# Merge gates and branch projections with tokens on the output's partitions, 512 weight columns moving

## The chip, the cores and the metric

The kernel runs on one core of a Trainium2 chip. The engines of that core work beside each other and are ordered by semaphores: TensorE (PE, matrix products; its weight loads are listed as PEld), VectorE (DVE), ScalarE (ACT), GpSimd (POOL) and SyncE (SP), which here issues every DMA. The metric is the device time of the whole kernel in microseconds, the median over runs.

## The reference

One layer of a hybrid block over 256 latent tokens and 256 context tokens of width 2048, in float32. The input is normalised and modulated, then one large projection feeds three mixers: neighbourhood attention, multi-scale pooling, and a two-directional RWKV-7 scan. Each mixer's 1024 channels are multiplied by SiLU of a gate. What the change touches is the end of the layer:

```python
b_na = y_na.astype(dt) * jax.nn.silu(keep(na_gate))
b_pool = y_pool.astype(dt) * jax.nn.silu(keep(pool_gate))
b_rw = y_rw.astype(dt) * jax.nn.silu(keep(rw_gate))
g_na, g_pool, g_rw = jnp.split(jax.nn.sigmoid(keep(merge_logits)), N_BRANCH, axis=-1)
merged = g_na * (b_na @ w_branch[0]) + g_pool * (b_pool @ w_branch[1]) + g_rw * (b_rw @ w_branch[2])
out = merged @ w_out
return x_lat + gate_l[:, None] * out, None
```

The merge logits are 3 x 2048 columns of the input projection, each branch projection is 1024 by 2048, the output projection 2048 by 2048. A final normalisation follows.

## The kernel before

Every float32 product is made of three products in a faster format: an operand is split into a rounded high part (a copy on ACT) and the rest (a subtraction on DVE), and high x high, high x low and low x high are summed in PSUM. The weights are split on the way: `split_unit` (L563) loads 128x512 values into a `raw` tile (7 buffers), and makes `whi` and `wlo` of it (5 buffers each). The normalised input lies split in 16 + 16 tiles, `hh` and `hl`, with channels on partitions and 512 tokens along the row (the latent ones are 256 to 511).

Four stages follow each other. The start makes the modulation and the first tiles. The mixers run up to about 1330 us: a table `todo` of column tiles (`column_tile`, L718) feeds attention, pooling and the scan. A column tile computes 128 output channels for 256 or 512 tokens: the weights are the stationary operand, the tokens move, in four units of 12 products. The 48 tiles of the merge logits depend on nothing and stand last in the table, so they fill PE whenever no other tile is ready; `merge_out` (L827) writes the tanh of each to memory (`md_`). The order of the work on PE is written out by the class `Order`: it keeps a clock of its own, runs the steps of attention and scan when their inputs should be there, and otherwise takes the next product of a unit from `units()` (L1008), which keeps three units loaded ahead. After the last attention step, 64 pieces of the gate weights `w_mg` (256 KB each, `wg`, L958) are loaded, one with each unit, and multiplied on PE in between (`mg`, L970).

Each finished branch piece (128 channels, 256 tokens) is stored to memory by `keep` (L764). The third stage reloads all three branches, 1 MB each through one buffer, and splits them (L1044 to L1048). Then, for each of 16 blocks of 128 output channels and each of the 3 branches, 24 products (`mm3`, L573) with the weights stationary and 256 tokens moving make the projection `br`; DVE multiplies by the gate (tanh + 1) and adds. The sum comes out with channels on partitions, as the output projection needs it (`mh`, `ml`). The last stage, the output projection, keeps tokens stationary and moves 512 columns of `w_out`; its weights reuse `hh` and `hl`.

Of the kernel before, what the change touches and what calls it, by code (L numbers as in the profile page):

```python
# [531 lines left out]
def hybrid_block(ctx, tc, x, cx, w_ms, w_st, w_in, w_mg, w_br, w_out, pool_w, icnt, wa, bias, rows, params, out, dbg=None):  # L532
# [20 lines left out]
    md_ = drp.tile([48, P, NT], F32, name="md_")  # L553
    bs = drp.tile([3, 8, P, NT], F32, name="bs")

    hh = [hp.tile([P, 512], F32R, name=f"hh{j}") for j in range(16)]
    hl = [hp.tile([P, 512], F32R, name=f"hl{j}") for j in range(16)]
# [4 lines left out]
    def split_unit(src):  # L562
# [3 lines left out]
        nc.sync.dma_start(raw, src)  # L566
# [6 lines left out]
    def mm3(acc, a, b, start, stop):  # L573

        nc.tensor.matmul(acc, a[0], b[0], start=start, stop=False)  # L575
        nc.tensor.matmul(acc, a[0], b[1], start=False, stop=False)  # L576
        nc.tensor.matmul(acc, a[1], b[0], start=False, stop=stop)  # L577
# [170 lines left out]
    with ExitStack() as mx:  # L748
# [15 lines left out]
        def keep(br, p, b):  # L764
            nc.sync.dma_start(bs[br, p], b)
# [61 lines left out]
        def merge_out(i, d):  # L827
            th = wp.tile([P, NT], F32, tag="th", bufs=1, name=f"mth{i}")
            nc.scalar.activation(th, d, AF.Tanh, scale=0.5)
            nc.sync.dma_start(md_[i], th)  # L830
# [174 lines left out]
        for i in range(48):  # L1005
            todo.append((None, tile_(MERGE + i, True, merge_out, i)))

        def units():  # L1008

            ready, cur, gates = [], [], gate_units()  # L1010
            while True:
                while len(ready) < AHEAD:
                    if not cur:
                        i = next((i for i, (ev, _) in enumerate(todo) if ev is None or O.has(ev)), None)
                        if i is None:
                            break
                        cur = todo.pop(i)[1]()
# [11 lines left out]

        O.add(side(), 0)  # L1030
# [5 lines left out]
    mark(nc, "bload")  # L1036
    bp = ctx.enter_context(tc.tile_pool(name="bp", bufs=1, reuse_waits="tile"))
    bx = ExitStack()
    bq = bx.enter_context(tc.tile_pool(name="bq", bufs=1, reuse_waits="tile"))
    tp = bx.enter_context(tc.tile_pool(name="tp", bufs=2, reuse_waits="tile"))  # L1040
    bh, bl = [], []
    for br in range(3):
        f = tp.tile([P, 8, NT], F32, tag="bf", bufs=1, name=f"bf{br}")
        nc.sync.dma_start(f, bs[br].rearrange("k p t -> p k t"))  # L1044
        h_ = bq.tile([P, 8, NT], F32R, name=f"bh{br}")
# [144 lines left out]
```

## Time and profile before

| | |
|---|---|
| time, median of 3 runs | 1597.64 us (1594.66 to 1600.06) |
| profiled execution: its time, its span | 1594.74 us, 1593.0 us |
| busy: PE, PEld, DVE, ACT, POOL | 1520.5, 1309.4, 1132.3, 815.9, 242.3 us |
| from the first to the last product on gate weights | 1178.7 to 1324.8 us |
| branch projections, from the first product to the output projection | 1350.9 to 1497.1 us |
| bytes moved, mean rate | 283.28 MB, 178 GB/s |

Times of the profile are microseconds from the span's start. A matrix product is drawn longer than its share of the engine, since products are pipelined; what one costs is seen from the distance of the starts. The DMA share is the mean busy share of the 16 DMA engines of the core.

### The profile page before, as it was taken

Reading aid. Unit: us, or ns where it says so; the run is one execution under the profiler, and the core shown is the slowest. Engines: PE = TensorE matmul, PEld = TensorE weight load, DVE = VectorE, ACT = ScalarE, POOL = GpSimd, SP = SyncE. Lnnn points to the kernel's source line nnn. Section 1 sums busy time; section 2 is a strip of 40 time slices with the busy share of each in tenths; the row PEclk is TensorE's granted clock in tenths of the full one; section 3 lists DMA queues with packets and bytes.
Section 4 is the critical chain, followed back from the end, with each engine's and each line's share of the span. In section 5 each row is a group of like instructions: output and inputs, shape, how many; then the busy total and the mean of one; then the engine's idle time right before and its main releaser. Section 6 shows DMA issues by size and latency. Waiting matters only on the chain.

```text
span 1593.0 us, 36719 instructions
## 1 busy us (share of the span) xinstructions
PE 1520.5 (95%) x13976; PEld 1309.4 (82%) x13976; DVE 1132.3 (71%) x2585; ACT 815.9 (51%) x1606; POOL 242.3 (15%) x441
## 2 busy tenths in 40 slices
PE   6999999999999999999999999899998999899997
PEld 4667788988887988888888887787887778899987
DVE  4224787898787787779779777777984444677774
ACT  5224653664664564366466446535743344444553
POOL 2222100330220150022024103002310200000000
PEclk9999999999999999999999999999999999999999
DMA  9997454435433544433434452443378788777882
GB/s 381 339 330 231 142 161 141 149 113 172 124 118 122 148 125 130 146 98 107 133 124 130 140 161 63 126 129 123 112 226 244 246 272 263 225 233 232 280 301 73
DMA packets 209809, 283.28 MB, mean 178 GB/s; under 512 B 67808, under 2 KB 114016, under 8 KB 205024
## 3 DMA queue, kind: packets, MB, share of 16 engines
q1 hardware_dynamic: 209632, 280.93, 55.1%
q8 instruction: 110, 1.80, 0.5%
q14 instruction: 67, 0.55, 0.1%
HBM read 262.24 MB, written 18.35 MB: 176 GB/s over the span
## 4 chain that ended last, share of the span: by engine, by line
PE 78%; DVE 9%; DMA 5%; ACT 4%; issue 2%; POOL 1%; SPq 1%; ACTq 0%; DVEq 0%; POOLq 0%
PE d L739 43%; PE br L575 3%; PE br L577 3%; PE br L576 3%; PE acc L663 2%; PE psm L615 2%; PE o L577 2%; PE o L575 2%; PE o L576 2%; DMA wg<-in_w_mg 2%; PE acc L669 2%; PE acc L666 2%; DVE wlo L570 1%; PE pu L388 1%; DMA bf<-bs 1%
## 5 line engine op out<-in xcount | busy, mean ns | idle before, releaser
L569 ACT CAST whi<-raw 128x512 fp32r<-128x512 f32 x584 | 358.5, 620 | 445.8 <-PE d L739 307.3
L739 PE MATMUL d<-hh,whi 128*128 128x256 f32 (+1 forms) x1952 | 578.7, 320 | 0.7 <-ACT whi L569 0.7
L739 PE MATMUL d<-hl,whi 128*128 128x256 f32 (+1 forms) x1952 | 552.4, 306 | 0.0
L570 DVE TENSOR_TENSOR wlo<-raw,whi 128x512 fp32r<-128x512 f32 x584 | 405.0, 701 | 176.1 <-ACT whi L569 123.5
L739 PEld LDWEIGHTS d<-hh,whi 128*128 128x128 f32 x1952 | 368.4, 189 | 44.1 <-issue 11.7
L739 PEld LDWEIGHTS d<-hl,whi 128*128 128x128 f32 x1952 | 369.3, 189 | 19.2 <-issue 1.6
L739 PE MATMUL d<-hh,wlo 128*128 128x256 f32 (+1 forms) x1952 | 362.3, 306 | 2.0 <-DVE wlo L570 2.0
L739 PEld LDWEIGHTS d<-hh,wlo 128*128 128x128 f32 x1952 | 286.6, 189 | 20.9 <-DVE wlo L570 2.4
L370 POOL TENSOR_SCALAR sg<-SV,G 64x64 f32<-64x64 f32 x192 | 108.3, 569 | 280.0 <-DVE SV L407 138.2
L575 PE MATMUL br<-bh,whi 128*128 128x256 f32 x384 | 108.9, 284 | 5.6 <-ACT bh L1047 5.6
L576 PE MATMUL br<-bl,whi 128*128 128x256 f32 x384 | 108.7, 283 | 1.5 <-DVE bl L1048 1.5
L577 PE MATMUL br<-bh,wlo 128*128 128x256 f32 x384 | 108.6, 283 | 0.0
L575 PEld LDWEIGHTS br<-bh,whi 128*128 128x128 f32 x384 | 73.3, 191 | 6.0 <-ACT bh L1047 5.8
L576 PEld LDWEIGHTS br<-bl,whi 128*128 128x128 f32 x384 | 73.2, 191 | 1.7 <-DVE bl L1048 1.7
L577 PEld LDWEIGHTS br<-bh,wlo 128*128 128x128 f32 x384 | 73.2, 191 | 0.0
L309 DVE TENSOR_TENSOR iM<-iA,iT 128x126 f32<-128x126 f32 (+22 forms) x248 | 63.4, 256 | 12.7 <-DMA iA<-dA 6.2
L311 DVE TENSOR_TENSOR iT<-iT,iM 128x126 f32<-128x126 f32 (+22 forms) x248 | 63.6, 257 | 6.6
L676 ACT ACTIVATE hh<-xT,md 128x256 fp32r<-128x256 f32 x32 | 17.5, 593 | 88.9 <-DVE md L635 88.9
L1118 DVE TENSOR_TENSOR hl<-rawo,hh 128x512 fp32r<-128x512 f32 x64 | 42.8, 690 | 21.5 <-ACT hh L1117 21.0
L1117 ACT CAST hh<-rawo 128x512 fp32r<-128x512 f32 x64 | 39.5, 621 | 33.0 <-PE o L577 23.3
L139 POOL MEMSET up<- 128x8 f32 x16 | 1.8, 112 | 345.4 <-PE mp L339 183.9
L624 DVE COPY ms<-psm 128x256 f32<-128x256 f32 x16 | 6.8, 425 | 65.1 <-PE psm L615 65.1
(283 smaller groups left out, 2335.7 us busy)
## 6 DMA issues: line engine op xcount, KB each, us to landing
raw<-in_w_in SPq DMA_DIRECT2D x488, 256.0 KB, 3.4
wm<-in_w_ms SPq DMA_DIRECT2D x32, 1024.0 KB, 6.6
raw<-in_w_br SPq DMA_DIRECT2D x96, 256.0 KB, 3.3
wg<-in_w_mg SPq DMA_DIRECT2D x64, 256.0 KB, 4.1
rawo<-in_w_out SPq DMA_DIRECT2D x64, 256.0 KB, 4.4
wst<-in_w_st SPq DMA_DIRECT2D x16, 448.0 KB, 7.3
md__79<-mth SPq DMA_DIRECT2D x48, 128.0 KB, 2.9
mth<-md__79 SPq DMA_DIRECT2D x48, 128.0 KB, 3.1
```

What stands on the lines that cost most here:

```text
L309: nc.vector.tensor_tensor(m, A[:, st:st + 1, st + 1:32].to_broadcast([128, ni, nt]), T[:, 0:ni, st:st + 1].to_broadcast([128, ni, nt]), AL ...
L311: nc.vector.tensor_tensor(T[:, 0:ni, st + 1:32], T[:, 0:ni, st + 1:32], m, ALU.add)
L370: nc.gpsimd.tensor_scalar(sg[hv[par], d], SV[hv[par], par, w, d], G[hv[par], gs[d][0], d:d + 1], None, ALU.mult)
L569: nc.scalar.copy(h, raw)
L570: nc.vector.tensor_tensor(l, raw, h.bitcast(F32), ALU.subtract)
L575: nc.tensor.matmul(acc, a[0], b[0], start=start, stop=False)
L576: nc.tensor.matmul(acc, a[0], b[1], start=False, stop=False)
L577: nc.tensor.matmul(acc, a[1], b[0], start=False, stop=stop)
L615: mm = nc.tensor.matmul(psm[j][32 * g:32 * g + 32, 0:256], cs[:, kt], wm[:, k], start=(kt < 4), stop=(kt >= 12), tile_position=(0, 32 * g))
L739: nc.tensor.matmul(box[0], w[m >= 8][:, 128 * i:128 * i + 128], x, start=(u == 0 and m == 0), stop=(u == 3 and m == 11))
L1117: nc.scalar.copy(hh[kt], raw)
L1118: nc.vector.tensor_tensor(hl[kt], raw, hh[kt].bitcast(F32), ALU.subtract)
```

## The change

The merge logits and the branch projections now have the output projection's form: 128 tokens are stationary, 512 weight columns move, and the results have tokens on partitions. A `group` is one block of 512 output channels for both halves of the tokens. It goes through 16 (merge) or 8 (branch) units; each unit is one 128-channel slice of the input with the weights of four neighbouring column tiles (four pieces of 128 columns per partition, out of the unchanged layout in memory). There are 12 merge groups in the place of 48 tiles and 4 groups per branch in the place of 48 blocks. A group holds two PSUM banks, one for each half of the tokens.

`keep` stores the branches already split. They are loaded into the places of the input (`hh`, `hl`) once the last merge group is on its way: those of attention and pooling with its units 7 to 14, those of the scan after its last piece is stored. The sums lie in the last input tiles. The first two branches' groups run as fillers (`late`) inside the mixers' stage; only the scan's branch is left for the stage behind, where four transposes per sum on PE bring it to channels on partitions. The gate weights come with two of three units instead of every unit. In `mm3` the second and third product change places.

```diff
-    md_ = drp.tile([48, P, NT], F32, name="md_")
-    bs = drp.tile([3, 8, P, NT], F32, name="bs")
+    md_ = drp.tile([12, 2, P, 512], F32, name="md_")
+    bs = drp.tile([3, 2, 8, P, NT], F32, name="bs")
...
-        nc.sync.dma_start(raw, src)
+        nc.sync.dma_start(raw.rearrange("p (n c) -> p n c", c=128) if len(src.shape) == 3 else raw, src)
...
+    def group(nk, src, st, bank, done):
+        acc, w = [None, None], {}
+        def unit_(k):
+            w[k] = split_unit(src(k))
+            def mult(k, t):
+                if k == 0:
+                    acc[t] = bank(t)
+                x = [a[:, 128 * t:128 * t + 128] for a in st(k)]
+                mm3(acc[t], x, w[k], k == 0, k == nk - 1)
+                if k == nk - 1:
+                    done(t, acc[t])
+                return 0.68
+            seq = [(k, 0)] + [(k - 1, 1)] * (k > 0) + [(k, 1)] * (k == nk - 1)
+            return [lambda a=a: mult(*a) for a in seq]
+        return [lambda k=k: unit_(k) for k in range(nk)]
...
+    def branch_load(i):
+        br, k = i // 4, 2 * (i % 4)
+        for e, y in enumerate((hh, hl)):
+            x = y[i] = hp.tile([P, 512], F32R, tag=f"h{'hl'[e]}{i}", name=f"b{'hl'[e]}{i}")
+            nc.sync.dma_start(x.bitcast(F32).rearrange("p (k t) -> p k t", k=2), bs[br, e, k:k + 2].rearrange("k p t -> p k t"))
+    def branch_src(br, c):
+        return lambda k: w_br[br, 4 * c:4 * c + 4, :, 128 * k:128 * k + 128].rearrange("n p c -> p n c")
...
         def keep(br, p, b):
-            nc.sync.dma_start(bs[br, p], b)
+            h = wp.tile([P, NT], F32R, tag="th", bufs=1, name=f"kh{br}_{p}")
+            nc.scalar.copy(h, b)
+            l = b.bitcast(F32R)
+            nc.vector.tensor_tensor(l, b, h.bitcast(F32), ALU.subtract)
+            nc.sync.dma_start(bs[br, 0, p], h.bitcast(F32))
+            nc.sync.dma_start(bs[br, 1, p], l.bitcast(F32))
...
+        def merge_group(i):
+            src = lambda k: w_in[MERGE + 4 * i:MERGE + 4 * i + 4, :, 128 * k:128 * k + 128].rearrange("n p c -> p n c")
+            return group(16, src, lambda k: (hh[k][:, 256:512], hl[k][:, 256:512]), dbank, lambda t, d: merge_out(i, t, d))
...
-        for i in range(48):
-            todo.append((None, tile_(MERGE + i, True, merge_out, i)))
+        for i in range(12):
+            todo.append((None, lambda i=i: merge_group(i)))
+        late = [lambda br=br, c=c: branch_group(br, c) for br in range(2) for c in range(4)]
...
-                        if O.has("side7") and gates:
-                            cur = [lambda u=u, g=gates.pop(0): u() + g() for u in cur]
                     ready.append(cur.pop(0)())
+                    if free is not None:
+                        if 0 <= free - 7 < 8:
+                            branch_load(free - 7)
+                        if free >= 20 and loads and O.has("rw7"):
+                            branch_load(loads.pop(0))
+                        free += 1
+                    n += 1
+                    if n % 3 and O.has("side7") and gates:
+                        ready[-1] = ready[-1] + gates.pop(0)()
...
-        f = tp.tile([P, 8, NT], F32, tag="bf", bufs=1, name=f"bf{br}")
-        nc.sync.dma_start(f, bs[br].rearrange("k p t -> p k t"))
...
+        def done(t, a):
+            nc.vector.scalar_tensor_tensor(th[t], th[t], 1.0, a, ALU.add, ALU.mult)
+            nc.vector.tensor_tensor(th[t], th[t], merged(t, c), ALU.add)
+            ps = psn.tile([P, 4, P], F32, tag="so"[t], name=f"mt{c}_{t}")
+            for i in range(4):
+                nc.tensor.transpose(ps[:, i], th[t][:, 128 * i:128 * i + 128], ident)
```

PE while gate weights stream, before: `d123` is a merge tile, `whi` and `wlo` the split weights, `hh0` and so on the input, `mg3` the gate products.

```order
L970 MATMUL mg3_17559<-wg3_0_7_17640,cs_74 32x256 x2
L739 MATMUL d123_17713<-hh0_81,whi465_17660 128x256
L739 MATMUL d123_17713<-hl0_97,whi465_17660 128x256
L739 MATMUL d123_17713<-hh1_82,whi465_17660 128x256
L739 MATMUL d123_17713<-hl1_98,whi465_17660 128x256
L739 MATMUL d123_17713<-hh2_83,whi465_17660 128x256
```

The same place in the changed kernel: `dg0` and `dg1` are the two halves of the tokens of a pooling-branch group, `bh5` and `bl5` the branch in the place of the input.

```order
L1043 MATMUL mg3_17419<-wg3_1_3_17622,cs_74 32x256 x2
L575 MATMUL dg0_17593<-whi534_17632,bh6_16832 128x512
L576 MATMUL dg0_17593<-whi534_17632,bl6_16834 128x512
L577 MATMUL dg0_17593<-wlo534_17633,bh6_16832 128x512
L575 MATMUL dg1_17608<-whi533_17618,bh6_16832 128x512
L576 MATMUL dg1_17608<-whi533_17618,bl6_16834 128x512
L577 MATMUL dg1_17608<-wlo533_17619,bh6_16832 128x512
L575 MATMUL dg0_17593<-whi535_17648,bh7_16848 128x512
```

A unit of 12 narrow products has become one of six wide ones, and what fills PE beside the gate products are now mostly branch groups, since more merge work stands ahead of them.

The DMA queue of SP at the same place, before (`raw` is a unit's weights, `md` the tanh going out):

```order
L566 DMA raw_17106<-in_w_in 128x512
L566 DMA raw_17148<-in_w_in 128x512
L830 DMA md__79<-mth_16833 128x256
L958 DMA wg_1_6_16855<-in_w_mg 128x2x256
L958 DMA wg_1_7_16888<-in_w_mg 128x2x256
L566 DMA raw_17169<-in_w_in 128x512
L566 DMA raw_17217<-in_w_in 128x512
L958 DMA wg_0_0_16919<-in_w_mg 128x2x256
```

And of the changed kernel, with the units 7 and following of the last merge group:

```order
L566 DMA raw_16714<-in_w_in 128x4x128
L611 DMA bh_16720<-bs 128x2x256
L611 DMA bl_16722<-bs 128x2x256
L566 DMA raw_16730<-in_w_in 128x4x128
L611 DMA bh_16736<-bs 128x2x256
L611 DMA bl_16738<-bs 128x2x256
L1031 DMA wg_1_0_16740<-in_w_mg 128x2x256
L566 DMA raw_16752<-in_w_in 128x4x128
L611 DMA bh_16758<-bs 128x2x256
L611 DMA bl_16760<-bs 128x2x256
L1031 DMA wg_1_1_16762<-in_w_mg 128x2x256
L566 DMA raw_16770<-in_w_in 128x4x128
```

The weights come in four pieces per partition, and the branch loads, which stood in a stage of their own, share the queue with weights and gate weights.

More of the change, by code (lines that the diff above doesn't have):

```diff
@@ L1028, in units @@
                     yield m()
+        loads = [8, 9, 10, 11]
         O.add(side(), 0)
@@ L1033, in hybrid_block @@
             O.run(units(), MOST, LEAST)
-    mark(nc, "bload")
+        for i in loads:
+            branch_load(i)
+    mark(nc, "merge")
     bp = ctx.enter_context(tc.tile_pool(name="bp", bufs=1, reuse_waits="tile"))
[L1038 to L1042, printed above, removed]
-        f = tp.tile([P, 8, NT], F32, tag="bf", bufs=1, name=f"bf{br}")
-        nc.sync.dma_start(f, bs[br].rearrange("k p t -> p k t"))
-        h_ = bq.tile([P, 8, NT], F32R, name=f"bh{br}")
-        l_ = bq.tile([P, 8, NT], F32R, name=f"bl{br}")
-        nc.scalar.copy(h_, f)
-        nc.vector.tensor_tensor(l_, f, h_.bitcast(F32), ALU.subtract)
-        bh.append(h_)
-        bl.append(l_)
+    bx = ctx.enter_context(tc.tile_pool(name="bx", bufs=2, reuse_waits="tile"))
@@ new lines, in last_branch, with done @@
+    def last_branch(c):
+        th = []
+        for t in range(2):
+            th.append(bx.tile([P, 512], F32, tag=f"mth{t}", name=f"mth{c}_{t}"))
+            nc.sync.dma_start(th[t], md_[8 + c, t])
+        def done(t, a):
+            nc.vector.scalar_tensor_tensor(th[t], th[t], 1.0, a, ALU.add, ALU.mult)
[3 more added lines that the diff above has]
+                nc.tensor.transpose(ps[:, i], th[t][:, 128 * i:128 * i + 128], ident)
+            o = (slice(None), slice(4 * c, 4 * c + 4), slice(128 * t, 128 * t + 128))
+            nc.scalar.activation(mh[o], ps, AF.Copy, scale=0.5)
+            nc.vector.scalar_tensor_tensor(ml[o], ps, 0.5, mh[o].bitcast(F32), ALU.mult, ALU.subtract)
+        pool_, tag = ((psd, "d"), (psf, "f"))[c % 2]
+        return group(8, branch_src(2, c), branch_st(2), lambda t: pool_.tile([P, 512], F32, tag=tag, name=f"br{c}_{t}"), done)
@@ L1075, in hybrid_block @@
+    for c in range(4):
+        for u in last_branch(c):
+            for m in u():
+                m()
     mark(nc, "out")
-    bx.close()
     tp = ctx.enter_context(tc.tile_pool(name="op", bufs=2, reuse_waits="tile"))
@@ L1116, in hybrid_block @@
                 nc.sync.dma_start(raw, w_out[cc, u, :, 512 * k:512 * k + 512])
+                if cc == 0:
+                    hh[kt] = hp.tile([P, 512], F32R, tag=f"hh{kt}", name=f"wh{kt}")
+                    hl[kt] = hp.tile([P, 512], F32R, tag=f"hl{kt}", name=f"wl{kt}")
                 nc.scalar.copy(hh[kt], raw)
```

70 lines of the change are left out of this document (42 added, 28 removed).

## The prediction

> **What bounds the kernel now.** I read the page's busy line and slices, then the chain by line.
>
> ```profile
> span 1593.0 us, 36719 instructions
> PE 1520.5 (95%) x13976; PEld 1309.4 (82%) x13976; DVE 1132.3 (71%) x2585; ACT 815.9 (51%) x1606; POOL 242.3 (15%) x441
> PE 78%; DVE 9%; DMA 5%; ACT 4%; issue 2%; POOL 1%; SPq 1%; ACTq 0%; DVEq 0%; POOLq 0%
> ```
>
> PE carries 78% of the chain; DVE, next by busy time, has over a quarter of the span free. So a gain has to be PE time, or a wait of PE. How much one product costs is read from starts, since the drawn lengths overlap. The timeline of PE gives, for the branches, for the output projection and for a key tile of the mixers:
>
> ```profile
> 1485.02 0.28 PE L575 MATMUL br<-bh,whi 128*128 128x256 f32 x1
> ...
> 1497.10 0.39 PE L575 MATMUL o<-hh,mh 128*128 128x512 f32 x1
> ...
> 1500.97 0.39 PE L577 MATMUL o<-hh,ml 128*128 128x512 f32 x1
> 377.64 0.39 PE L739 MATMUL d<-hh,whi 128*128 128x512 f32 x1
> ...
> 391.64 0.40 PE L739 MATMUL d<-hh,whi 128*128 128x512 f32 x1
> ```
>
> From the first row to the second there are 102 products of 256 columns in 12.08 us: 118.4 ns each. The 17 of 512 columns behind them take 3.87 us: 227.6 ns each. The key tile's 60 take 14.00 us: 233.3 ns each. Two narrow ones (236.9 ns) thus cost little more than one wide one.
>
> Where PE waits, and how full the DMA is, stand in the table of stretches (columns: stretch, length, then busy us and instructions of PE, weight load, DVE, ACT, POOL; granted clock, DMA share, GB/s):
>
> ```profile
> 0.00:100.00 100.00, 85.59 (x639) 58.94 (x640) 34.66 (x85) 35.83 (x54) 25.94 (x28) 1.00 0.94 353
> 300.00:1100.00 800.00, 774.93 (x7646) 671.41 (x7645) 638.62 (x1545) 440.36 (x907) 149.29 (x288) 1.00 0.42 128
> 1185.00:1250.00 65.00, 58.30 (x615) 46.42 (x617) 35.21 (x92) 20.18 (x38) 6.47 (x12) 0.97 0.83 254
> 1250.00:1315.00 65.00, 64.26 (x630) 51.49 (x627) 31.40 (x67) 27.44 (x53) 5.93 (x12) 1.00 0.80 258
> 1330.00:1365.00 35.00, 26.19 (x212) 25.40 (x211) 18.90 (x26) 16.97 (x25) 0.00 (x0) 0.95 0.84 273
> 1365.00:1497.00 132.00, 132.00 (x1103) 131.87 (x1102) 100.13 (x187) 65.62 (x112) 0.00 (x0) 0.99 0.73 228
> 1500.00:1590.00 90.00, 84.95 (x421) 72.12 (x419) 53.24 (x90) 42.27 (x78) 0.00 (x0) 0.98 0.60 207
> ```
>
> In the mixers (300 to 1100) the DMA is at 0.42. It is full, 0.80 to 0.83, only where the gate weights stream (1185 to 1315), and there PE idles 6.70 + 0.74 = 7.4 us. At the reload of the branches (1330 to 1365) PE idles 8.8 us and has a lower clock.
>
> **The change part by part.** The sum is made against the profiled execution, 1594.7 us with its span of 1593.0; the median shown, 1597.6, is 2.9 above it.
>
> *Width.* 48 x 48 merge and 48 x 24 branch products, 3456 narrow ones, become 1728 wide ones. The output projection has the roles that they get (tokens stationary, weights moving), so I take its 227.6: 1728 x (236.9 - 227.6) = 16 us less. By the key tile it is 1728 x 3.6 = 6 us, the other bound.
>
> The Trainium skill (TensorE: Matmul & The Clock Gate, Back-to-back issue gap) gives N / 2.4 + 2.5 ns for a warm product: 109.2 and 215.8 ns, so only 1728 x 2.6 = 4.5 us, and the sum below would end 11.5 us higher. The rows above are longer than both of its figures, and by more for the narrow one; the measurement decides.
>
> *The reload of the branches* (L1044 to L1048) goes. The instructions on its tile, and who waited:
>
> ```profile
> L1047 ACT CAST bh<-bf x3: 1897/1908/1914, 1341.3 to 1362.3; 128x2048 fp32r<-128x2048 f32 x3
> L1048 DVE TENSOR_TENSOR bl<-bf,bh x3: 2291/2291/2292, 1343.3 to 1364.3; 128x2048 fp32r<-128x2048 f32 x3
>   PE br L575: 5.6, 1
> ```
>
> PE gets back 8.8 us and about 1.7 us of clock (35 us at 0.95): 10.5 us. The loads now come as 24 transfers (L611 of the changed kernel) among the fillers, and the splitting moves into keep: 24 copies and subtractions on 128x256, and 24 more stores. At nothing: ACT and DVE have time (440 and 639 of 800 us). keep shares one buffer with the SiLU gates, so ACT may wait there for a store to land; before, 48 tanh tiles waited so in that buffer and now use others. Uncovered, it is 24 x 2.9 us, by the first row here.
>
> ```profile
> bs<-gplg SPq DMA_DIRECT2D x8, 128.0 KB, 2.9
> md__79<-mth SPq DMA_DIRECT2D x48, 128.0 KB, 2.9
> ```
>
> *Transposes.* 32 of them (L1145 of the changed kernel) bring the sum back to channels on partitions:
>
> ```profile
> L906 PE MATMUL pt<-ident,sl 128*128 128x128 f32 x128 | 19.6, 276 | 0.9 <-DVE st L899 0.9
> ```
>
> 19.6 / 128 x 32 = 4.9 us more. What they wait for (two DVE instructions) is covered by the next group's units, which stand ahead of them on PE, and for the last group by the output projection's first.
>
> *The stall at the gate weights*, 7.4 us, goes if nothing replaces it. So **PE alone** gives -16 - 10.5 - 7.4 + 4.9 = -29 us.
>
> *The price: the DMA.* A unit's 256 KB came as 128 pieces of 2 KB and now comes as 512 pieces of 512 B (four tiles of w_in or w_br side by side); the gate weights come two per three units, and 24 branch transfers and 24 tanh reads or writes and gate rows fall among them. Before, that part runs from the first gate product to the last:
>
> ```profile
> L970 PE MATMUL mg<-wg,cs x256: 379/391/403, 1178.7 to 1324.8; 128*32 128x256 f32 x128
>   DMA wg<-in_w_mg: 15.2, 17
> DMA  8788989748889586798877785686788887899988
> GB/s 216 226 278 265 266 270 297 197 76 272 281 267 338 189 277 225 256 282 259 267 227 230 253 280 187 206 267 203 244 256 246 302 231 271 245 353 375 322 275 273
> ```
>
> (the last two rows: its 147 us in 40 slices.) What 512 B cost there I work out from the table: 353 GB/s at 0.94, all in pieces of 8 KB but few, are 42.6 ns per KB on one of 16 engines, 349 ns a piece; 207 GB/s at 0.60, pieces of 2 KB, are 46.4 ns per KB, 95 ns a piece. The line through both has 10 ns + 42.3 ns per KB: 53 ns for 1 KB, 32 ns for 512 B. So 256 KB on a full DMA take 0.76, 0.84 and 1.01 us in pieces of 2 KB, 1 KB and 512 B; this line is my estimate.
>
> By the order, between first and last gate product stand 558 wide products now and 744 narrow ones before. PE alone would need 146.1 - 7.4 - 744 x 0.1184 + 558 x 0.2276 = 178 us. The DMA has 93 units (94 us), 64 gate and 24 branch transfers of 1 KB pieces (74 us), and some 24 of 2 KB (18 us): 187 us with a little rest, 9 over PE's time. From there to the output projection PE needs 172.3 - 159.1 (192 + 1152 narrow) - 10.5 + 62.1 (273 wide) + 4.9 = 70 us; the DMA has 45 units and about 35 others of 2 KB, 72 us. Bounds: at a share of 0.94 these are 199 and 77, so 21 + 7 = 28 us over PE; at the 375 GB/s of one slice, where the line has about 327 for a half-and-half mix of 1 and 2 KB, they shrink to 163 and 63, none over. I take 12 + 4 = 16 us: a little above the line's 9 + 2, as transfers are issued one by one on SP behind waits for buffers.
>
> Sum: -29 + 16 = -13, so 1581.7 for such an execution and 1584.6 if the median stays 2.9 above it; I say 1583, between them.
>
> **The rivals.**
>
> *The DMA keeps up.* Then -29: 1566 to 1569. For it, the slices at 353 and 375 GB/s; against it, these are two of 40, and none is of 512 B pieces.
>
> *The DMA sets the pace and the kernel is slower.* Place: from the first gate product to the output projection; price: 259 us of transfers, divided by the share reached, less PE's 248. It decides below a share of 0.94, where the overrun passes 29 us. At the 0.87 between the 0.83 of the gate part and the 0.94 of the start it is 298 - 248 = 50, so +21: 1616 to 1619. For it: PE already waits for gate weights at 0.81, in 17 places. Against it: at 0.81 the DMA was not asked for more.
>
> The Trainium skill (DMA: Bandwidth & Descriptors, Latency and other measured facts) has a rule on this side: rows of HBM at a pitch of 512 KiB gave 207 GB/s, at 2 MiB 164. The four pieces of a partition lie 512 KiB or 1 MiB apart here, though neighbouring partitions still lie as close as before; no run here shows it yet. By its 207 the units alone take 177 us instead of 140. The same page's Specifications name 512 B as enough for line rate, which speaks for the first rival.
>
> *The width gives 6 us rather than 16, and the DMA costs its 28 at a share of 0.94*, or a group's 16 units hold both banks (about 22 us, where a tile took four units) and push other work behind: -19 + 16 to -19 + 28, so 1592 to 1604, no change that can be told.
>
> **How the numbers follow.** The forecast (a gain, partly eaten) has 0.43, the DMA keeping up 0.15, the slower one 0.26, the last 0.16. This kernel's measurement tells 0.3%, 4.8 us, from no change, so faster is below 1592.8, slower above 1602.4. Faster: nearly all of 0.43 and 0.15, 0.56; the same 0.17; slower 0.27. The forecast's own range is 1570 to 1592; the range to hold 8 in 10 runs from 1561, the first rival with a little more from the width, to 1617, the second.
>
> **What would show it.** Products of the merge and branch groups start 0.228 us apart where nothing waits (width); no stall ahead of the branch products (reload); from the first gate product to the last some 190 us, with a DMA share of 0.9 or more, and waits of PE for the splits and of these for raw tiles (price). Under 180 us, the first rival holds; over 210, the second. The forecast is wrong in kind if the part before the first gate product, where the DMA is at 0.42, gets longer than the added units explain: 897 wide products against 1368 narrow ones, 42 us, by which the first gate product moves from 1179 to about 1221.

## The result, and the profile after

The changed kernel takes 1638.97 us (median of 4 runs, 1637.07 to 1644.63), the kernel before 1596.15 us beside it (4 runs, 1592.34 to 1600.06). The ratio is 1.0273, interval [1.0248, 1.0297]: 43 us slower, where 13 us faster was forecast, and outside the range.

From the page of the changed kernel, its span, its busy line and its chain of waits:

```profile
span 1637.9 us, 33130 instructions
PE 1542.8 (94%) x12280; PEld 1211.7 (74%) x12280; DVE 1125.4 (69%) x2558; ACT 812.5 (50%) x1593; POOL 241.3 (15%) x441
PE 54%; DMA 6%; DVE 4%; ACT 4%; issue 1%; SPq 0%; POOL 0%; ACTq 0%; DVEq 0%; POOLq 0%
```

PE is still the busiest engine, and the span is 44.9 us longer. (The chain could be followed back only to 492 us here, so its shares add up to 69% and can't be set beside those of the kernel before.) The stretches (columns as before) and the products on gate weights:

```profile
300.00:1100.00 800.00, 763.65 (x6851) 623.96 (x6851) 631.40 (x1534) 437.46 (x895) 143.69 (x287) 0.99 0.44 131
1179.00:1275.00 96.00, 85.56 (x742) 72.77 (x741) 71.18 (x170) 46.45 (x88) 14.52 (x21) 0.95 0.58 167
1275.00:1470.00 195.00, 179.66 (x1027) 113.26 (x1026) 88.28 (x157) 69.25 (x120) 10.69 (x20) 0.99 0.92 268
1470.00:1540.00 70.00, 69.61 (x303) 53.76 (x302) 50.73 (x79) 34.88 (x59) 0.00 (x0) 1.00 1.02 300
```

```profile
L1043 PE MATMUL mg<-wg,cs x256: 379/403/636, 1275.2 to 1469.5; 128*32 128x256 f32 x128
```

From the first gate product to the last it takes 194.3 us, at a DMA share of 0.92; the forecast said some 190 and 0.9 or more. But the first gate product stands at 1275.2, not at 1221. In the mixers, where the DMA is at 0.44 (0.42 before), PE is busy for 763.65 of 800 us, 11.3 less than before.

To see where the time went, I took from the trace the start of every PE product and the distance to the next start. A column tile's or a group's product has a bare price, the median distance inside long runs: 0.1175 us narrow (256 columns), 0.2333 us wide (512). What its distance has above that is called **lost** here: waits, interruptions by other products, and half clock (stretches with a granted clock of 0.5). Three stages of the profiled executions, in us:

| | to the first gate product: bare, lost, all else | to the output projection: bare, lost, gate products, all else | output |
|---|---|---|---|
| before | 711 + 60 + 246 = 1017 | 245 + 28 + 28 + 17 = 318 | 88 |
| after | 760 + 95 + 258 = 1114 | 194 + 32 + 23 + 14 = 264 | 90 |

(The first stage is counted from 161 us, when the mixers are under way.) The second stage is 54.8 us shorter, as forecast (190 + 74 = 264 us). The first is 96.5 us longer, where 42 were forecast. That difference, 54 us, is the whole miss but for 3 us in the output stage.

Such figures come from one execution each. Two kernels below, `e10_half_gates` and `e17_reload`, are the changed kernel up to the first gate product; there it stands at 1283.4 and 1273.1 us, and 99 and 91 us are lost ahead of it. So a difference of less than some 10 us in this stage shows nothing by itself.

### The profile page after: what moved, and what is told of

It is laid out like the page before. It is cut to its first block, busy times and chain, and to the rows that moved or that the text cites. A ratio compares the mean times of both kernels' runs of the same rounds, so it can differ in the third digit from the quotient of the medians.

```text
span 1637.9 us, 33130 instructions
## 1 busy us (share of the span) xinstructions
PE 1542.8 (94%) x12280; PEld 1211.7 (74%) x12280; DVE 1125.4 (69%) x2558; ACT 812.5 (50%) x1593; POOL 241.3 (15%) x441
## 4 chain that ended last, share of the span: by engine, by line
PE 54%; DMA 6%; DVE 4%; ACT 4%; issue 1%; SPq 0%; POOL 0%; ACTq 0%; DVEq 0%; POOLq 0%
PE d L783 23%; PE dg L575 5%; PE dg L577 4%; PE dg L576 4%; DMA raw<-in_w_br 3%; DMA raw<-in_w_in 2%; PE o L577 2%; PE o L576 2%; PE o L575 2%; ACT whi L569 1%; PE pu L388 1%; PE px L374 1%; PE pS L398 1%; DVE wlo L570 1%; PE br L575 1%
## 5 line engine op out<-in xcount | busy, mean ns | idle before, releaser
L783 PE MATMUL d<-hh,whi 128*128 128x256 f32 (+1 forms) x1184 | 373.9, 335 | 15.4 <-ACT whi L569 15.2
L783 PE MATMUL d<-hl,whi 128*128 128x256 f32 (+1 forms) x1184 | 363.6, 326 | 0.0
L783 PEld LDWEIGHTS d<-hh,whi 128*128 128x128 f32 x1184 | 226.7, 191 | 42.2 <-ACT whi L569 17.8
L783 PE MATMUL d<-hh,wlo 128*128 128x256 f32 (+1 forms) x1184 | 245.4, 326 | 0.2 <-DVE wlo L570 0.2
L783 PEld LDWEIGHTS d<-hl,whi 128*128 128x128 f32 x1184 | 227.3, 192 | 18.6 <-issue 0.9
L783 PEld LDWEIGHTS d<-hh,wlo 128*128 128x128 f32 x1184 | 183.3, 192 | 19.1 <-issue 0.7
L575 PE MATMUL dg<-whi,hh 128*128 128x512 f32 x384 | 166.6, 434 | 10.0 <-ACT whi L569 7.3
L577 PE MATMUL dg<-wlo,hh 128*128 128x512 f32 x384 | 153.8, 401 | 1.7 <-DVE wlo L570 1.6
L576 PE MATMUL dg<-whi,hl 128*128 128x512 f32 x384 | 152.0, 396 | 0.0
L576 PEld LDWEIGHTS dg<-whi,hl 128*128 128x128 f32 x384 | 72.7, 189 | 10.3
```

The lines of the kernel that those rows point to most:

```text
L576: nc.tensor.matmul(acc, a[1], b[0], start=False, stop=False)
L577: nc.tensor.matmul(acc, a[0], b[1], start=False, stop=stop)
L783: nc.tensor.matmul(box[0], w[m >= 8][:, 128 * i:128 * i + 128], x, start=(u == 0 and m == 0), stop=(u == 3 and m == 11))
```

## The experiments

Three theories for the first stage stood at the start. **S** (widened to **Q** later): SP serves one queue in order, and transfers that wait on it for other engines hold the weight loads behind them. **P**: the 512-byte pieces land late everywhere. **G**: groups of 16 units on both banks push other work behind. What had put S first is one place in the mixers, where a merge group ends and a column tile of attention begins. SP's queue, then ACT, in the timeline of the changed kernel:

```profile
407.19 0.33 SPq L879 DMA_DIRECT2D md__79<-mth  x1
408.84 1.27 SPq L315 DMA_DIRECT2D dT<-iT  x2
410.21 0.64 SPq L879 DMA_DIRECT2D md__79<-mth  x1
410.90 0.94 SPq L566 DMA_DIRECT2D raw<-in_w_in  x2
412.18 4.80 SPq L321 DMA_DIRECT2D AT<-dT  x8
```

```profile
406.57 0.60 ACT L878 ACTIVATE mth<-dg 128x512 f32<-128x512 f32 x1 [1.71 <-PE dg L577]
407.96 0.60 ACT L878 ACTIVATE mth<-dg 128x512 f32<-128x512 f32 x1 [0.79 <-PE dg L577]
415.37 0.62 ACT L569 CAST whi<-raw 128x512 fp32r<-128x512 f32 x1 [6.81 <-DMA raw<-in_w_in]
```

The stores of the group's two tanh tiles can't go before ACT has made them, at 407.2 and 408.6. The raw loads of the next units stand behind them and go out at 410.90; ACT waits 6.81 us for one, and PE stops for 5.4 us. But the second store goes out only at 410.21, behind two transfers of the scan's inverse (`dT`, issued from 408.84 on, once DVE has made `iT`): the place shows both kinds of wait. SP's waits for a store, up to the first gate product, before and after:

```profile
SPq L830 <- ACT mth L829: 34.4, 17, 8.4
```

```profile
SPq L879 <- ACT mth L878: 74.3, 15, 17.4
SPq L813 <- ACT kh L810: 37.5, 19, 7.6
```

### Stores off SP, whole pieces, both; and the width alone

`e1_stores`:

```diff
-            nc.sync.dma_start(md_[i, t], th)
+            nc.scalar.dma_start(md_[i, t], th)
-            nc.sync.dma_start(bs[br, 0, p], h.bitcast(F32))
-            nc.sync.dma_start(bs[br, 1, p], l.bitcast(F32))
+            nc.scalar.dma_start(bs[br, 0, p], h.bitcast(F32))
+            nc.scalar.dma_start(bs[br, 1, p], l.bitcast(F32))
```

> The changed kernel, but the stores of the merge logits' tanh tiles and of the kept mixer outputs (high and low part) are started from ACT's DMA queue instead of SP's, so that no raw weight load stands behind a store that still waits for ACT or DVE. The output is the same. Theory S (SP's queue is served in order, and the stores hold back the raw loads of the next fillers, which starves PE and sends it into half clock): the first gate product comes at 1230 to 1245 us instead of 1275, the half-clock stretches before it fall from eight to two or three, and the median falls by 30 to 40 us, to 1600 to 1608. Theory P (the 512-byte pieces make the raw loads late everywhere): SP's waits go away but the loads still land late; under 10 us gained, 1629 or more. Theory G (a group's 16 units hold both banks and push the column tiles back): no gain, 1634 to 1642.

`e2_contig` (`w_mr` and `w_br` are laid out on the host so that a unit is one block):

```diff
-            src = lambda k: w_in[MERGE + 4 * i:MERGE + 4 * i + 4, :, 128 * k:128 * k + 128].rearrange("n p c -> p n c")
+            src = lambda k: w_mr[i, k]
-        return lambda k: w_br[br, 4 * c:4 * c + 4, :, 128 * k:128 * k + 128].rearrange("n p c -> p n c")
+        return lambda k: w_br[br, c, k]
```

> The changed kernel, but the input layout holds the merge columns and the branch weights so that a unit of a group reads 2 KB in one piece per partition instead of four pieces of 512 bytes. The instructions are the same in the same order. Theory P: the first gate product moves from 1275 to 1230 to 1245 us and the part from the first to the last gate product shrinks from 194 to about 178 us (PE's own time there); median 1580 to 1595. Theory S: the first gate product stays at 1265 or later and only the gate part shrinks; median 1617 to 1627. Theory G: as S. If DMA wasn't what set the gate part's pace, 1634 to 1642.

`e3_both` has both edits.

> Both edits together: stores from ACT's queue, 2 KB pieces. If S holds for the mixers and the pieces only cost the gate part, the gains add: 30 to 40 and about 16 us, 1582 to 1592, under the kernel before by 4 to 14 us. If P holds alone, the same as the kernel with 2 KB pieces, within 5 us. If G holds, 1617 to 1627.

`e4_halves`:

```diff
-        nc.tensor.matmul(acc, a[0], b[0], start=start, stop=False)
...
+        for i, (u, v) in enumerate(((0, 0), (1, 0), (0, 1))):
+            whole = (start and i == 0) or (stop and i == 2) or not halves
+            for c in (slice(None),) if whole else (slice(0, 256), slice(256, 512)):
+                nc.tensor.matmul(acc[:, c], a[u], b[v][:, c], start=start and i == 0, stop=stop and i == 2)
```

> The changed kernel, but each product of a group that moves 512 weight columns is made as two products of 256 columns with the same stationary tile (only the first and the last product of each accumulation stay whole); loads, order and buffers are the same. It asks what the width alone is worth. If the width is worth the 9.3 ns a pair that the prediction took (two narrow products 236.9 ns, one wide 227.6): 900 pairs in the mixers cost 8 us, the rest hides behind the transfers or adds up to 8 more; 1647 to 1655. If undisturbed wide and narrow products run at the same pace per column (0.233 against two of 0.1175 us): 2 ns a pair, under 3.5 us in all, 1637 to 1643.

| | median us | ratio to before | first gate product at | lost ahead of it | to the last gate product |
|---|---|---|---|---|---|
| changed kernel | 1638.97 | 1.0273 [1.0248, 1.0297] | 1275.2 | 95 | 194 |
| e1_stores | 1631.95 | 1.0225 [1.0188, 1.0261] | 1267.3 | 85 | 194 |
| e2_contig | 1636.08 | 1.0240 [1.0207, 1.0273] | 1268.8 | 91 | 191 |
| e3_both | 1630.53 | 1.0212 [1.0188, 1.0237] | 1267.4 | 86 | 193 |
| e4_halves | 1666.88 | 1.0440 [1.0412, 1.0468] | 1292.2 | 106 | 197 |

P falls: with 2 KB pieces the first gate product comes 6 us sooner, less than the spread named above, the second stage is 3.5 us shorter, and the median can't be told from the changed kernel's (the intervals overlap). S is right in kind and far too large: the loss inside runs of narrow column tiles falls from 28.7 us (30.1 and 24.1 in the two repeats of this stage) to 13.3, but the median by 7, not by 30 to 40, and the two intervals still overlap at their edges. e3_both, 1.4 us below e1_stores, is clear of the changed kernel; none of its expectations held (it is 5.6 us below e2_contig, where P alone allowed 5). Something else then stands in the loads' way. SP's waits of e1_stores up to its first gate product:

```profile
SPq L566 <- DMA md__79<-mth: 41.2, 16, 6.0
SPq L315 <- DVE iT L311: 17.9, 6, 10.4
```

A raw load now waits for a raw buffer that a tanh tile holds until its store has landed; and the inverse's transfers still wait on SP for DVE. At the place shown above, SP's timeline of e1_stores has:

```profile
408.19 1.33 SPq L315 DMA_DIRECT2D dT<-iT  x2
409.63 2.47 SPq L566 DMA_DIRECT2D raw<-in_w_in  x3
```

With both stores gone, the raw loads go out 1.1 us after the column tile's first product instead of 3.1, still behind the inverse, and PE stops for 3.8 us instead of 5.4.

The halves missed on both sides. Undisturbed, two halves cost what a whole product costs. The timeline of PE in e4_halves:

```profile
388.78 0.40 PE L578 MATMUL dg<-whi,hl 128*128 128x256 f32 x2
389.01 0.40 PE L578 MATMUL dg<-wlo,hh 128*128 128x256 f32 x2
389.25 0.40 PE L578 MATMUL dg<-whi,hh 128*128 128x256 f32 x2
389.48 0.40 PE L578 MATMUL dg<-whi,hl 128*128 128x256 f32 x2
389.71 0.39 PE L578 MATMUL dg<-wlo,hh 128*128 128x256 f32 x2
```

Four pairs in 0.93 us are 0.2325 a pair, against 0.2333 for one wide product. Ahead of the first gate product the groups' products take 241.6 us in halves and 238.3 whole. So the width is worth next to nothing as a pace. Yet the kernel is 28 us slower: two starts of PE lie more than 1.75 us apart 23 times instead of 15, and PE runs 82 us at half clock instead of 41 (both up to its last product); 41 us more at half speed cost up to 20 of the 28. Why products half as long let PE stop more often isn't settled by these runs.

### The queue's order

`e5_first` raises the priority of the raw loads, `e6_before_first` does so in the kernel before, `e7_stores_first` adds it to e1_stores:

```diff
-        nc.sync.dma_start(raw.rearrange("p (n c) -> p n c", c=128) if len(src.shape) == 3 else raw, src)
+        with tc.high_priority(offset=100):
+            nc.sync.dma_start(raw.rearrange("p (n c) -> p n c", c=128) if len(src.shape) == 3 else raw, src)
```

> The changed kernel with one edit: the raw weight loads of the fillers get a higher priority in the order of SP's queue, so that several of them stand ahead of the stores and of the inverse's transfers that they followed before. PE's order is untouched. Theory Q (whatever waits on SP, store or transfer of the scan, holds the loads behind it; stores off the queue alone gave 7 us of about 35): the first gate product comes at 1240 to 1258 us instead of 1275 and the median falls to 1612 to 1625. Theory B (the loads are late for want of buffers: a whi tile is held one unit longer by a group and two raw tiles by the tanh): under 5 us gained, 1633 or more. Theory D (moving loads ahead delays the inverse's transfers and the scan): slower, 1642 or more.

> The control: the kernel before with the same edit of the loads' priority. Theory Q says that its loads aren't held up by much (its waits of whi on a raw load are 14 us in the mixers, 8 times): within 4 us of the kernel before, 1592 to 1602. If the edit gains here what it gains in the changed kernel, the queue's order isn't what the change made worse.

> Both: stores on ACT's queue and loads first on SP. Theory Q: what is left of the loads' lateness goes, the first gate product at 1235 to 1255 us, median 1605 to 1620. Theory B: as with the stores alone, 1629 to 1636.

`e8_ahead4`:

```diff
-NRAW, NSP, AHEAD = 7, 5, 3
+NRAW, NSP, AHEAD = 7, 5, 4
```

> The changed kernel with loads asked for four units ahead of PE instead of three (PE's order shifts a little, since a filler is chosen one unit earlier). Theory Q: 1.4 us more lead covers part of the stalls, 5 to 15 us gained, 1622 to 1634. Theory B: with five whi tiles, of which a group holds one longer, the fourth unit ahead finds no tile; 1634 to 1643.

The kernel before doesn't feel it: 1597.51 us, ratio 1.0009 [0.9996, 1.0023]. The changed one gets slower every time: 1654.61 (1.0357 [1.0323, 1.0391]), 1654.05 (1.0373 [1.0343, 1.0404]) and 1649.52 us (1.0326 [1.0293, 1.0360]). Yet the loads do come earlier: the loss inside runs of narrow tiles is 10.1, 11.5 and 6.5 us, and all that is lost ahead of the first gate product 79, 77 and 82 instead of 95. Theory D of e5_first (the scan is delayed, slower) describes it; the ranges given for the other two were missed. The rest of the scan's and attention's products take 269, 268 and 271 us instead of 258, and with the loads first (e5_first, e7_stores_first) the gate weights come late. Who PE's gate products waited for in e5_first (in the changed kernel this wait is 0.4 us):

```profile
L1044 PE MATMUL mg<-wg,cs x256: 378/403/637, 1269.4 to 1474.9; 128*32 128x256 f32 x128
...
  DMA wg<-in_w_mg: 35.7, 23
```

With the loads first, what is gained ahead is given back at the next transfer in the same queue; in e8_ahead4 it is given back in the scan. The profiled executions of these three (1645, 1648 and 1641 us) are 6 to 9 us shorter than the medians, so that much of the slowing is in no trace.

`e9_queues` is e1_stores with the inverse's four kinds of transfers (`dA`, `iA`, `dT`, `AT`) started by POOL:

```diff
-            nc.sync.dma_start(A[64 * j:64 * j + 64], dA.rearrange("q n i s t -> (q n i) s t"))
+            nc.gpsimd.dma_start(A[64 * j:64 * j + 64], dA.rearrange("q n i s t -> (q n i) s t"))
```

> The changed kernel with the stores on ACT's queue and also the transfers of the scan's inverse (its matrices to DRAM and back) on POOL's queue, so that almost nothing but weight loads is left on SP. If one in-order queue for loads, stores and the inverse's transfers is what costs the mixers their time (theory Q), neither the loads nor the scan come late now: the narrow column tiles lose under 8 us between products instead of 28.7, the scan's products take no longer, the first gate product comes at 1240 to 1255 us instead of 1275, median 1605 to 1622. If POOL starts these transfers late, or the cost lies in the order of PE's work, no gain over the stores alone: 1630 or more.

1667.17 us, 1.0422 [1.0388, 1.0455]. The loads are freed (11.0 us lost inside runs of narrow tiles), but the other products take 286 us: the inverse's transfers take longer from issue to landing. The DMA table, the changed kernel first:

```profile
dT<-iT SPq DMA_DIRECT2D x16, 128.0 KB, 2.7
AT<-dT SPq DMA_DIRECT2D x64, 32.0 KB, 2.1
```

```profile
dT<-iT POOLq DMA_DIRECT2D x16, 128.0 KB, 4.1
AT<-dT POOLq DMA_DIRECT2D x64, 32.0 KB, 2.8
```

So this run frees the loads but puts another delay on the scan, and can't show what an undisturbed SP queue would be worth.

Which of the stores it is was asked with one kind moved at a time, and in the kernel before (`e13_mth`: the tanh tiles; `e14_keep`: the kept outputs; `e16_before_stores`: `md_[i]` of the kernel before):

> The changed kernel with only the stores of the tanh tiles on ACT's queue (the kept outputs' stores stay on SP). With both off SP, the time lost between fillers before the first gate product fell from 95 to 85 us, and of that the loss inside runs of narrow column tiles from 28.7 to 13.3. If the tanh stores at a group's end hold the loads (SP waits 74 us for them, 15 times): at most 17 us lost inside runs, median 1630 to 1636. If the kept outputs' stores do (37.5 us, 19 times): over 22 us, 1635 to 1642.

> The changed kernel with only the kept outputs' stores on ACT's queue: the mirror of the run before it. Tanh stores to blame: over 22 us lost inside runs of narrow column tiles, median 1635 to 1642. Kept outputs to blame: at most 17 us, 1630 to 1636.

> The control: the kernel before with its tanh stores on ACT's queue. SP waits there 34.4 us for them in 17 waits, and the loss inside runs of narrow column tiles is 5.1 us in all, so next to nothing can be gained: 1592 to 1601. If it falls by 5 us or more, the stores cost the kernel before as well, and it is a version faster than both.

The loss inside runs of narrow tiles is 17.0 us without the tanh stores on SP, 24.4 without the kept outputs', 13.3 without both, 28.7 with both. The tanh stores are to blame: with them on SP this loss is 24.1 to 30.1 us in five kernels that are alike up to there but for the size of the pieces and the kept outputs' stores (the changed one, e2_contig, e10_half_gates, e14_keep, e17_reload), and off SP 13.3 to 17.0 us in four (e1_stores, e3_both, e13_mth, e18_three). So they make some 11 of the 24 us that it grew by; what the kept outputs' stores cost is within this spread. The medians, 1637.29 (1.0262 [1.0233, 1.0291]) and 1646.12 us (1.0303 [1.0266, 1.0340]), can't be told from the changed kernel's; that of e13_mth misses its expectation by 1 us, that of e14_keep by 4. The kernel before becomes 1594.68 us, 0.9979 [0.9966, 0.9993]: 0.2% faster, the only version here that beats both kernels. Its trace doesn't show why: 65 us are lost ahead of its first gate product, against 60.

### The size of a group

`e12_before_coarse` takes the merge tiles of the kernel before four at a time; `e11_fine` gives the changed kernel half as large groups on one bank; `e15_fine_stores` adds the stores on ACT's queue:

```diff
-        for i in range(48):
-            todo.append((None, tile_(MERGE + i, True, merge_out, i)))
+        for i in range(12):
+            todo.append((None, lambda i=i: [u for k in range(4) for u in column_tile(MERGE + 4 * i + k, True, lambda d, n=4 * i + k: merge_out(n, d))]))
```

```diff
-            todo.append((None, lambda i=i: merge_group(i)))
+            todo.append((None, lambda i=i: merge_fine(i)))
...
+                    for m, (a, b) in enumerate(((0, 0), (1, 0), (0, 1))):
+                        nc.tensor.matmul(box[0][:, 256 * t:256 * t + 256], x[a], w[b][:, c], start=(kt == 0 and t == 0 and m == 0),
```

> The kernel before, but its merge tiles are taken four at a time, 16 units that no other column tile can part (narrow, one bank each, as before; the gate weights at three units in two, since fewer units are left for them). By the order, 4092 narrow products stand before the first gate product, against 3672, as many as in the changed kernel (4098 narrow products' worth). Bare pace then puts the first gate product at 1179 + 49 = 1228 us, and 9 more if 176 of the mixers' other products move ahead too. Theory G: the lost time between fillers rises from 60 to 85 us or more, first gate product at 1255 to 1275 us. Theory Q (the tanh and the new stores do it, not the size): 1228 to 1245 us. The end isn't compared, because the gate weights come denser.

> The changed kernel, but the merge logits are made in groups of 256 columns: 24 groups of 8 units, both token tiles in the two halves of one bank, 12 narrow products a unit (the tokens stay on the output's partitions, the layout gives a unit 2 KB a partition; the branches stay as changed). By the order, 3816 narrow products' worth of column work stands before the first gate product, against 3672 in the kernel before and 4098 in the changed one. If the size of a group, 16 units on both banks, is what delays the mixers (theory G): the lost time between fillers falls back from 95 to 60 to 70 us, the first gate product comes at 1200 to 1215 us, median 1600 to 1615. If it is the queue's order (theory Q): 1215 to 1245 us, median 1620 to 1638. If width were worth what was predicted, its loss alone costs 8 us more than under G.

> The fine groups (256 columns, 8 units, one bank) with both kinds of stores on ACT's queue. If the two causes add (order by the groups' size, loads held by the stores): time lost before the first gate product from 79.5 to about 65 us, first gate product near 1205 us, median 1615 to 1624. If the loss only moves behind the first gate product, as it did with the loads put first: 1628 to 1636.

The gate products of e12_before_coarse, then of e11_fine:

```profile
L970 PE MATMUL mg<-wg,cs x256: 379/391/403, 1246.8 to 1355.8; 128*32 128x256 f32 x128
```

```profile
L1066 PE MATMUL mg<-wg,cs x256: 379/403/636, 1217.2 to 1426.6; 128*32 128x256 f32 x128
```

In e12_before_coarse only 66 us are lost ahead of the first gate product (60 before), and 7.3 instead of 5.1 inside runs of narrow tiles. So size alone doesn't make the loads late, and G as stated, a loss between the fillers, falls. But size does move work: the first gate product comes 68 us later, of which 49 are fillers at their bare price and 13 other products (168 more of them) that now stand ahead of it. Fewer units are then left to run beside the gate and branch transfers, and 44 us instead of 28 are lost in the second stage. One run took 1624.81 us, 27 above the kernel before beside it; the denser gate weights are in that.

In e11_fine the first gate product comes 58 us earlier than in the changed kernel (32 of them are the bare price of merge work that now stands behind it), just inside what Q expected, but the end comes only 6 us earlier: 1633.40 us, 1.0221 [1.0199, 1.0243], as under Q. 80 us are lost ahead and 43 in the second stage. With the stores off SP (1636.24 us, 1.0236 [1.0206, 1.0266]) the first gate product comes at 1208 us and the two are 73 and 51: the loss moved behind the first gate product.

### The second stage

`e10_half_gates` leaves out the loads of half the gate weights (zeros stand in their place, so the gate's values change); `e17_reload` spreads the branch reloads; `e18_three` is e3_both with that:

```diff
+                if k % 4 < 2:
+                    nc.sync.dma_start(wg, w_mg[cc, k, :, :, 256 * h:256 * h + 256])
+                else:
+                    nc.gpsimd.memset(wg, 0.0)
```

```diff
-                        if 0 <= free - 7 < 8:
-                            branch_load(free - 7)
+                        if 7 <= free < 23 and free % 2:
+                            branch_load((free - 7) // 2)
```

> The changed kernel with half of the gate weights not loaded (POOL sets those tiles to zero; the products run all the same): 8.4 MB less to move between the first and the last gate product. If bytes set the pace there (it took 194 us, with 259 to 307 GB/s moved): 178 to 184 us and a median of 1623 to 1630. If waits in SP's queue behind tanh and gate stores set it, or PE itself: 190 us or more, median 1634 or more.

> The changed kernel, but the eight reloads of the branch inputs (512 KB each, high and low part) go out at every second unit instead of at every unit. Between 1345 and 1400 us a unit of 1.4 us asks for 256 KB of weights, 512 KB of branch inputs and two thirds of 256 KB of gate weights, over 600 GB/s where the trace shows about 300 moved; PE loses 12 to 18 us there in stalls of 0.9 to 3 us, and neither smaller gate loads nor 2 KB pieces mended it. If this burst sets the loss: 5 to 10 us gained, first to last gate product 184 to 189 us instead of 194, median 1628 to 1634. If tanh, reload of the tanh and gate stores on SP set it: under 3 us, 1636 to 1642.

> Stores on ACT's queue, 2 KB pieces and the slower reload together. If the parts add (7, 3 and 5 to 10 us): 1618 to 1626, and still slower than the kernel before by over 1%, since the order of the work (column tiles behind groups of 16 units, fewer units left behind the mixers) is untouched. If they only move the loss: 1628 to 1636.

The worst 50 us of that stage, in the changed kernel, e2_contig, e10_half_gates and e17_reload:

```profile
1350.00:1400.00 50.00, 38.18 (x162) 20.92 (x163) 15.11 (x22) 13.33 (x23) 0.00 (x0) 0.97 1.03 307
```

```profile
1350.00:1400.00 50.00, 41.25 (x187) 24.55 (x186) 18.24 (x27) 15.78 (x26) 0.00 (x0) 0.97 0.94 314
```

```profile
1350.00:1400.00 50.00, 40.80 (x175) 22.89 (x173) 15.37 (x23) 13.37 (x23) 2.97 (x6) 0.93 1.02 302
```

```profile
1350.00:1400.00 50.00, 41.50 (x174) 24.90 (x175) 16.42 (x24) 13.97 (x24) 0.00 (x0) 0.90 1.09 324
```

Each eases the load on the DMA, and each time it still moves just over 300 GB/s there and PE still stands 8.5 to 9.2 us of the 50 (11.8 in the changed kernel). From first to last gate product these take 191, 190 and 192 us instead of 194; the medians are 1636.08, 1638.52 (1.0249 [1.0226, 1.0272]) and 1638.86 us (1.0283 [1.0253, 1.0312]). So neither piece size nor gate bytes nor the burst of reloads sets this by itself. e18_three takes 1625.11 us (1.0202 [1.0163, 1.0241]), within the expectation's first range, but not by its sum: the reload, put at 5 to 10 us, gave nothing alone. The three edits together mend 11 us of the 43 by the ratios, 14 by the medians.

## Why the prediction was wrong, step by step

*What bounds the kernel.* Right: PE's products are the same work in both kernels, and the time is that work plus what is lost around it. Up to the output projection 89 us are lost before and 128 after. The change had to lower that sum, and raised it by 39.

*Width, 16 us with 6 as the other bound.* Wrong: the other bound was nearer the price. Wide products in the groups start 0.2333 us apart, like the key tile's in the same stage, while the output projection keeps its 0.227 in both kernels. In the timeline of PE of the changed kernel:

```profile
391.67 0.40 PE L575 MATMUL dg<-whi,hh 128*128 128x512 f32 x1
...
407.53 0.39 PE L577 MATMUL dg<-wlo,hh 128*128 128x512 f32 x1
407.76 0.28 PE L783 MATMUL d<-hh,whi 128*128 128x256 f32 x1
...
410.13 0.63 PE L783 MATMUL d<-hh,wlo 128*128 128x256 f32 x4
```

68 wide products take 15.86 us (0.2332 each), 20 narrow ones 2.37 us (0.1185). That makes 3 to 7 us in all, by the median or by this mean; I had taken the row of another stage because the roles of the operands looked alike. (That the narrow row exceeds its 109.2 ns by more than the wide one its 215.8 holds as a share, 8.4% against 5.5%, not in ns, 9 against 12.)

*Reload, stall at the gate weights, price of the DMA: -10.5 - 7.4 + 16.* The stage came out as forecast, 264 us from the first gate product to the output projection and 263.6 measured, but by luck: the change of width and of order was worth 51 us there by the bare prices, not the 58 in the forecast, and all the rest fell by 3 us where these terms and the transposes add up to 3 more. The reason for the 16 was wrong in part: at most 3.5 us of it are the 512-byte pieces, since that is what whole pieces give back there. The line of prices rests on pieces of 8 KB in the first 100 us; 2320 of the 5944 packets there are smaller. And the second rival's 138 units take 175 us at its 207 GB/s, not 177.

*Transposes, 4.9 us.* 2.9 us by the distances of their starts.

*The part before the first gate product* is the step that failed, and the prediction had named it as the sign that the forecast would be wrong in kind. It gave 42 us to 897 wide against 1368 narrow products; 96.5 were measured. The 54 between are: 7 for the pace (49 bare); 9 for 176 products of the scan and attention that now stand ahead of the first gate product (they cost nothing in the end); 3.5 by which those products are slower; and 35 lost. Of the 35, 24 lie inside runs of narrow column tiles, 5 inside runs of the groups, and 7 at 275 interruptions instead of 254. That the tanh tiles' stores on SP make some 11 of the 24 is shown by e1_stores, e3_both, e13_mth and e18_three beside the five kernels that keep them there. For the rest, raw buffers held by tanh tiles and the inverse's transfers ahead of the loads are seen on SP, and what they cost was not tested alone. These amounts include half clock: 37.5 us of it ahead of the first gate product against 6.8, which costs up to 19 us instead of 3 (44.4 and 27.3 us in e10_half_gates and e17_reload, 10.2 and 13.7 in e6_before_first and e16_before_stores).

*keep's split, priced at nothing* and at 24 x 2.9 us uncovered: the wait feared was ACT's in the shared buffer. What came was SP's: its stores wait 37.5 us for ACT, with raw loads behind them. I had named what stands behind the waiting instruction on ACT and not on SP.

*The rivals.* The slower one came out on the right side for the wrong reason: it said a gate part over 210 us, and that was 194. The last one, in which a group's 16 units push other work behind (about 22 us), named a real effect, but no place for it: in e12_before_coarse, one run 27 us slower with the denser gate weights in it, the loss lies in the second stage for the most part. None had the loads late in the mixers.

What stays open: about 30 us of the 43 that no edit removed. Each kernel that lost 73 to 82 us ahead of the first gate product (e5, e7, e8, e11, e15) gave it back behind it or in the scan. Of all that lost under 90 us there, only e18_three also has a clearly shorter second stage (258 us against 264), and it is still 32 us above the kernel before. Whether a schedule exists that avoids both is open.

## What to carry to other kernels

Where a change leaves the bounding engine's work the same, ask first what it puts into the in-order queue that feeds that engine: a store that has to wait for its producer at the end of a group holds every load behind it, however empty the DMA is. Moving such stores to another queue is worth a trial, but here it gave back only 7 of 43 us: other waits in the same queue, for buffers and for the scan, were left. Price a new form of an instruction by the nearest row of its own stage, not by a better row elsewhere. And a larger unit of work isn't free even when the sum is equal: it moves the rest of the program, and, as e12_before_coarse suggests, the cover that was left for later transfers is used up early.

## What the runs showed of the hardware

**Half clock after a stop of 2 us.** The granted clock falls to half for 3.4, 6.8 or 10.2 us once PE has stopped for about 2 us (10.2 us in e4_halves and e17_reload). Stretches of 3.4 us of the changed kernel around the stop at 410:

```profile
406.70:410.10 3.40, 3.40 (x26) 3.18 (x25) 1.84 (x9) 1.07 (x2) 0.00 (x0) 1.00 0.21 78
410.10:413.50 3.40, 0.66 (x6) 0.45 (x4) 0.00 (x0) 0.00 (x0) 0.00 (x0) 1.00 0.92 214
413.50:416.90 3.40, 0.86 (x4) 0.86 (x5) 0.69 (x1) 0.78 (x2) 0.00 (x0) 0.53 0.75 161
416.90:420.30 3.40, 3.40 (x18) 3.40 (x18) 1.80 (x4) 0.46 (x1) 0.00 (x0) 0.50 0.63 149
```

After the stop PE is busy again, and still at 0.50 for 3.4 us. Ahead of the first gate product of the changed kernel eight such stretches follow stops of 1.9 to 5.6 us (by the distance of two starts); in the kernel before there is one, and a second at 1222 us. All starts of such stretches in one execution lie on one grid of 3.41 us, and it seems that whether a stop of 2 us is followed by one depends on where in the grid it falls: 6 of 15 stops of more than 1.75 us weren't, one of 2.03 us at 604 among them, while one of 2.02 us at 906 was.

The Trainium skill (TensorE: Matmul & The Clock Gate, What's actually happening) has the clock gated by a free-running window of 3413 ns. This case's grid agrees. Its idle state is entered after an idle window; here windows with PE at work were enough (0.66 of 3.40 us above, 1.82 of 3.41 us from 205.5 on). In e1_stores two windows in a row with 1.6 us were not, though a stop of 3.9 us lay across both; what exactly counts isn't shown.

**The DMA moved about as much in the second stage whatever the pieces**: with a unit's 256 KB in 512 pieces of 512 bytes 307 GB/s at a share of 1.03, in 128 of 2 KB 314 GB/s at 0.94. The pieces changed the share and hardly the rate. (The share adds up the packets' times and can pass 1.) The Trainium skill (DMA: Bandwidth & Descriptors, Latency and other measured facts) gives 207 GB/s for rows at a pitch of 512 KiB; the four pieces of a partition lie 512 KiB or 1 MiB apart, though neighbouring partitions are close together, and this case shows nothing of that kind.

**Wide products have two paces in one program**: 0.2333 us in groups, in the scan's branch behind the mixers and in key tiles, 0.227 in the output projection, of the same shape and type. What makes the 3% wasn't tried.
